# The first two column blocks of a convolution's input product share each quarter of x, in two accumulators

## The chip, the core and the metric

One Trainium2 chip, of which the kernel uses one core. The metric is the device time of one execution in microseconds (us), median of three runs. TensorE is written PE in the profile (PEld is its loading of weights), VectorE is DVE, ScalarE is ACT, GpSimd is POOL and SyncE is SP.

## What is computed

A trunk of two residual layers on x of 256 tokens by 2048 channels, all in float32. Layer 0 mixes tokens with a Conformer convolution, layer 1 with a state space; each is followed by a dense MLP. The change is in the first step of layer 0, `h @ w_in`, and in what surrounds it:

```python
def rms_norm(x, g):
    xf = x.astype(jnp.float32)
    y = xf * lax.rsqrt(jnp.mean(xf * xf, axis=-1, keepdims=True) + EPS)
    return (y * g.astype(jnp.float32)).astype(x.dtype)
...
def conv_module(h, w_in, b_in, dw, dw_b, ln_g, ln_b, w_out, b_out):
    u = h @ w_in + b_in
    a, gate = jnp.split(u, 2, axis=-1)
    v = a * jax.nn.sigmoid(gate)
    v = lax.conv_general_dilated(
        v, dw[:, None, :], window_strides=(1,),
        padding=[(CONV_WIDTH - 1, 0)],
        dimension_numbers=("NWC", "WIO", "NWC"),
        feature_group_count=D_MODEL) + dw_b
    v = layer_norm(v, ln_g, ln_b)
    v = jax.nn.silu(v)
    return v @ w_out + b_out
```

`w_in` is 2048 by 4096, and the depthwise convolution has 31 taps per channel.

## The kernel before

Every weight matrix is read once from HBM in steps of 1 MiB. A step lands in a tile `raw` (three buffers), and is split in two halves h = 0, 1, 2, ...: ACT writes the rounded part `hi` (line 118), and DVE, or POOL for the steps in `pool_lo`, the rest `lo` (line 125); there are four buffers of each. PE then makes three products per tile of weights (`mm_g`, lines 211 to 213: hi by the high part of x, hi by its low part, lo by its high part), so that the result is that of float32.

x comes in four quarters of 512 channels (`setup`). A quarter is transposed on PE (`xt`, line 254, two tiles of four transposes), scaled by the norm's weights on ACT and split on DVE into `hT` (lines 258 and 259). The RMS factor of the tokens is worked out from sums of squares (`junk`, `ssq`), raised to the power -0.5 on POOL, spread to all partitions by a product (`bc`, line 296), and applied after the product, in `gate`.

`conv_in` has 16 column blocks c of 128 + 128 columns (value and gate). A block needs 2048 channels, two steps, four halves and 96 products, in one accumulator `acc` of which there are two. Its end is `gate` (lines 446 to 448): DVE multiplies `acc` by the RMS factor, ACT makes the sigmoid `ga`, DVE writes v into `vT`, and `acc` is free. Blocks 0 to 11 then go through `depthwise`: 30 operations `cv` on DVE (line 829), the last of which writes `vT`. Blocks 12 to 15 (`PACKED`) do it on PE: v is copied in shifted form into `R` (for block 15 by 8 copies on DVE, line 470, and 8 on ACT, line 468), 32 small products make `pk` (line 484), and DVE finishes them. `centre` (line 569) takes a shift from four finished blocks at once, ACT squares them (`sq`), and PE adds both up into `stat` (line 539), from which `lst` and `tot` make the layer norm. Then comes `conv_out`.

The order on each engine is set when the program is built, by a scheduler that takes what is ready by its own estimate of times; `behind(ins)` puts one instruction after another, and `high_priority` brings one forward. On the chip each engine keeps that order and waits where an operand is missing. Transfers of x and of the weights are issued one behind the other on SP's queue (`fetch`, line 92), a quarter of x and a half step of weights in turn; the small vectors of the layer (`dwr`) are issued on POOL's queue behind `pow_ins`, so after the RMS factor.

```python
for n in range(NS):
    s = slice(n * 512, (n + 1) * 512)
    self.fetch(self.x[:, :, s], xv[:, :, s])
    self.load(n // 2, n % 2)
```

## Time and profile before

| | |
|---|---|
| median of three runs | 1987.88 us (1987.52 to 1989.23) |
| profiled execution | 1987.94 us, its span 1986.2 us |
| PE busy | 1966.6 us, 99% of the span |
| DVE busy | 1400.9 us, 71% |
| ACT busy | 952.1 us, 48% |
| POOL busy | 275.0 us, 14% |
| HBM read | 400.08 MB, 219 GB/s over the span |

The span counts from the first instruction; what lies outside it is 1.7 us. A row of the timeline gives the start in us from there, the time from the start to the end of what it merges, engine, line, operation, tiles and count; in brackets stands how long the engine was idle before, and what ended that. A matmul's printed duration holds its way through the array, so the pace of PE is read from the starts of neighbours. The stretch up to 230 us of the span is the one that the change touches: the first 38 us hold blocks 0 and 1, at 214 us block 15 ends, and at 236 us `conv_out` begins.

### The profile page before, as it was taken

The numbers are of one execution on the slowest core, as the hardware profiler recorded it, in microseconds if no ns is written. First come the engines' busy times: TensorE is split into PE (matmuls) and PEld (weight loads), VectorE is DVE, ScalarE is ACT, GpSimd is POOL, SyncE is SP. The second block draws the span as 40 slices with busy tenths as digits, with TensorE's granted clock in tenths as the row PEclk, the third lists the DMA queues.
The fourth block names the chain that finished last, engine by engine and source line by source line (L and its number), as shares of the span: only waits on it lengthen the run. The fifth ranks groups of instructions, "written<-read, shape, count | busy, mean of one in ns | idle before, by whom it ended". The sixth has DMA issues, their size and how long they took to land.

```text
span 1986.2 us, 28885 instructions
## 1 busy us (share of the span) xinstructions
PE 1966.6 (99%) x11604; PEld 1686.1 (85%) x11604; DVE 1400.9 (71%) x1903; ACT 952.1 (48%) x1179; POOL 275.0 (14%) x252
## 2 busy tenths in 40 slices
PE   8999999999999999999999999999999999999998
PEld 8999788888888888888888788888888888888887
DVE  6899798888777777777558847565555565655555
ACT  6444655544444544444445445454444454444444
POOL 3998300000000221222010000000000000000000
PEclk9999999999999999999999999999999999999999
DMA  8768458677686877877898865665656666666653
GB/s 225 192 184 219 135 185 267 205 227 244 201 255 196 215 230 251 264 247 239 319 308 296 304 216 185 191 191 190 191 191 191 191 191 191 190 213 191 191 191 128
DMA packets 317030, 428.49 MB, mean 216 GB/s; under 512 B 9761, under 2 KB 211553, under 8 KB 313537
## 3 DMA queue, kind: packets, MB, share of 16 engines
q1 hardware_dynamic: 301120, 384.85, 61.4%
q0 software_dynamic: 12352, 37.49, 6.3%
q10 hardware_dynamic: 3424, 4.30, 0.8%
q8 instruction: 91, 1.49, 0.3%
q14 instruction: 43, 0.35, 0.1%
HBM read 400.08 MB, written 34.91 MB: 219 GB/s over the span
## 4 chain that ended last, share of the span: by engine, by line
PE 95%; DVE 1%; DMA 1%; issue 1%; POOL 1%; SPq 0%; ACT 0%; ACTq 0%; POOLq 0%; DVEq 0%
PE acc L199 24%; PE acc L222 15%; PE acc L223 15%; PE acc L224 15%; PE acc L202 12%; PE acc L213 3%; PE acc L212 3%; PE acc L211 3%; PE pk L484 1%; DMA Vt<-Vd 0%; PE kp L1113 0%; SPq L92 0%; POOL lo L125 0%; PE xw L1254 0%; DMA raw<-in_conv_w_in_dram 0%
## 5 line engine op out<-in xcount | busy, mean ns | idle before, releaser
L118 ACT ACTIVATE hi<-raw 128x1024 fp32r<-128x1024 f32 x672 | 711.3, 1060 | 952.4 <-PE acc L224 507.2
L125 DVE TENSOR_TENSOR lo<-raw,hi 128x1024 fp32r<-128x1024 f32 x611 | 747.0, 1225 | 505.3 <-ACT hi L118 501.1
L199 PE MATMUL acc<-hT,hi 128*128 128x512 f32 x2048 | 514.4, 393 | 0.0
L199 PEld LDWEIGHTS acc<-hT,hi 128*128 128x128 f32 x2048 | 368.9, 189 | 68.0 <-issue 1.6
L222 PE MATMUL acc<-hi,rT 128*128 128x512 f32 x992 | 387.2, 391 | 0.0
L223 PE MATMUL acc<-lo,rT 128*128 128x512 f32 x992 | 386.4, 390 | 0.0
L224 PE MATMUL acc<-hi,rT 128*128 128x512 f32 x992 | 386.0, 389 | 0.0
L202 PEld LDWEIGHTS acc<-hT,lo 128*128 128x128 f32 x2048 | 279.6, 190 | 20.0
L202 PE MATMUL acc<-hT,lo 128*128 128x256 f32 x2048 | 286.4, 282 | 0.0
L222 PEld LDWEIGHTS acc<-hi,rT 128*128 128x128 f32 x992 | 186.3, 188 | 40.0 <-issue 1.6
L224 PEld LDWEIGHTS acc<-hi,rT 128*128 128x128 f32 x992 | 186.3, 188 | 38.7
L223 PEld LDWEIGHTS acc<-lo,rT 128*128 128x128 f32 x992 | 186.3, 188 | 38.1 <-issue 0.2
L125 POOL TENSOR_TENSOR lo<-raw,hi 128x1024 fp32r<-128x1024 f32 x60 | 142.9, 2402 | 31.9 <-ACT hi L118 31.8
L211 PE MATMUL acc<-hT,hi 128*128 128x256 f32 x512 | 145.8, 285 | 0.9 <-ACT hi L118 0.9
L212 PE MATMUL acc<-hT,hi 128*128 128x256 f32 x512 | 145.5, 285 | 0.3 <-DVE hT L259 0.3
L213 PE MATMUL acc<-hT,lo 128*128 128x256 f32 x512 | 145.3, 286 | 0.3 <-POOL lo L125 0.3
L829 DVE SCALAR_TENSOR_TENSOR cv<-vT,dw,cv 128x256 f32<-128x256 f32 x348 | 141.2, 481 | 2.2 <-ACT cv L527 1.7
L820 DVE TENSOR_TENSOR x<-x,acc 128x1024 f32<-128x1024 f32 (+1 forms) x72 | 83.6, 1161 | 28.1 <-PE acc L224 22.0
L211 PEld LDWEIGHTS acc<-hT,hi 128*128 128x128 f32 x512 | 98.6, 193 | 3.1 <-issue 1.6
L222 PE MATMUL acc<-hi,yT 128*128 128x512 f32 x256 | 101.1, 395 | 0.0
L223 PE MATMUL acc<-lo,yT 128*128 128x512 f32 x256 | 99.9, 390 | 0.6 <-DVE lo L125 0.6
L212 PEld LDWEIGHTS acc<-hT,hi 128*128 128x128 f32 x512 | 98.5, 193 | 2.2 <-issue 1.6
(280 smaller groups left out, 1722.5 us busy)
## 6 DMA issues: line engine op xcount, KB each, us to landing
raw<-in_mlp_w_up_dram SPq DMA_DIRECT2D x128, 1024.0 KB, 5.8
raw<-in_mlp_w_down_dram SPq DMA_DIRECT2D x128, 1024.0 KB, 5.2
raw<-in_ssm_w_glu_dram SPq DMA_DIRECT2D x32, 1024.0 KB, 5.5
raw<-in_conv_w_in_dram SPq DMA_DIRECT2D x60, 512.0 KB, 5.6
raw<-in_conv_w_out_dram SPq DMA_DIRECT2D x16, 1024.0 KB, 5.1
Vd<-bv POOLq DMA_DIRECT2D x16, 512.0 KB, 6.3
Md<-Kd POOLq DMA_DIRECT2D x32, 256.0 KB, 6.7
Wt<-Wd SPq DMA_DIRECT2D x8, 1024.0 KB, 9.4
```

The source lines that it names most:

```text
L118: self.nc.scalar.activation(hi, sl, AF.Copy)
L125: ins = eng.tensor_tensor(out=lo, in0=sl, in1=hi.bitcast(F32), op=ALU.subtract)
L199: mm(accs[m], lhsT=hi[:, kk, cs[m]], rhs=xT(k0 + kk), start=first and kk == 0, stop=False)
L202: mm(accs[m][:, 0:T], lhsT=lo[:, kk, cs[m]], rhs=xT(k0 + kk)[:, 0, :], start=False, stop=last and kk == 3)
L211: mm(accs[m], lhsT=hi[:, kk, c], rhs=x[:, 0, :], start=first and kk == 0, stop=False)
L212: mm(accs[m], lhsT=hi[:, kk, c], rhs=x[:, 1, :], start=False, stop=False)
L213: mm(accs[m], lhsT=lo[:, kk, c], rhs=x[:, 0, :], start=False, stop=last and kk == 3)
L222: mm(acc[:, b, :], lhsT=ak[:, 0, t], rhs=hi[:, kk, :], start=first and kk == 0, stop=False)
L223: mm(acc[:, b, :], lhsT=ak[:, 0, t], rhs=lo[:, kk, :], start=False, stop=False)
L224: self.mm_last = mm(acc[:, b, :], lhsT=ak[:, 1, t], rhs=hi[:, kk, :], start=False, stop=last and kk == 1)
L820: return self.nc.vector.tensor_tensor(out=out, in0=a, in1=b, op=op)
L829: return self.nc.vector.scalar_tensor_tensor(out=out, in0=a, scalar=s, in1=b, op0=op0, op1=op1)
```

## The change

Blocks 0 and 1 are no longer worked one after the other with the whole of x. Their four steps now hold one quarter of x's channels each, for block 0 in the first half and for block 1 in the second, so a quarter of x is used for 24 products into one accumulator and 24 into the other. Both accumulators stay open until the fourth quarter, and both gates follow then. From block 2 on nothing is different in the code.

With it, the first quarter of x and of block 0's weights come in two pieces each; transposing a quarter (`quarter`), the sums of squares (`sums`), the RMS factor (`norm`), and its spreading with the small vectors' transposes (`spread_norm`, `vectors`) are called from `run_steps` at set halves (`early`), behind the split before them; the vectors' transfers start when x's second quarter has landed (`go`) in place of the RMS factor; 8 products of `ones` and twice 3 of `ident` go ahead of the first product (`warm`, `keep_warm`); and ACT's tables are loaded by two one-column operations (`ld`).

```diff
-        for n in range(NS):
+        for p in range(2):
+            s = slice(p * 256, (p + 1) * 256)
+            self.fetch(self.x[:, :, s], xv[:, :, s])
+            self.load(0, 0, p)
+        self.load(0, 1)
+        for n in range(1, NS):
             s = slice(n * 512, (n + 1) * 512)
             self.fetch(self.x[:, :, s], xv[:, :, s])
-            self.load(n // 2, n % 2)
+            if n < NS - 1:
+                self.load(n)
...
+        warm = self.acc2("warm")[:, 0, 0:P]
+        for _ in range(8):
+            nc.tensor.matmul(warm, lhsT=self.ones, rhs=self.ones, start=True, stop=True)
...
-        for n in range(NS):
-            self.to_features(self.x, self.mix0, 4 * n, 4)
-        for n in range(NS):
-            self.sumsq(ssq, n, True)
-        self.rstdB = self.bcast_tok(self.rstd_tok(ssq))
+        for k in (0, 2):
+            self.spread = self.to_features(self.x, self.mix0, k, 2)
+            self.keep_warm(3, self.xt, warm)
...
+        self.early = {1: lambda: quarter(1), 3: lambda: quarter(2), 4: norm, 5: lambda: quarter(3), 6: spread_norm}
+        go = nc.gpsimd.tensor_copy(out=self.small.tile([P, 1], F32, tag="go", name="go", bufs=1), in_=self.x[:, 0, 512:513])
...
-            with self.behind(self.pow_ins):
+            with self.behind(go):
                 nc.gpsimd.dma_start(out=rows[r:r + n, :], in_=ap.rearrange("(k p) -> k p", p=P))
...
-        for c in range(KB):
+        for s in range(NS):
+            def consume(hi, lo, half, s=s):
+                if s == 0:
+                    st[half] = self.acc2()
+                A = st[half][:, :, 0:T]
+                hi, lo = (t.rearrange("p k h c -> p k (h c)") for t in (hi, lo))
+                self.mm_g([A[:, 0], A[:, 1]], self.hT, hi, lo, 4 * s, s == 0, s == NS - 1)
+                if s == NS - 1:
+                    self.gate(half, A)
+            self.add([w[:, 4 * s:4 * s + 4, :, c * P:(c + 1) * P] for c in range(2)], [P, 8, 2, P], consume)
+        for c in range(2, KB):
```

PE's first instructions in the kernel before (`mt` is the norm's weights, `xt` a tile of transposed x, `acc` the accumulator):

```order
L323 MATMUL mt<-ident,m_78 128x16
L254 MATMUL xt<-ident,x 128x128 x8
L211 MATMUL acc<-hT,hi 128x256
L212 MATMUL acc<-hT,hi 128x256
L254 MATMUL xt<-ident,x 128x128 x8
L213 MATMUL acc<-hT,lo 128x256
```

and in the changed one:

```order
L352 MATMUL warm<-ones 128x128 x8
L357 MATMUL mt<-ident,m_78 128x16
L276 MATMUL xt<-ident,x 128x128 x4
L211 MATMUL warm<-ident 128x128 x3
L276 MATMUL xt<-ident,x 128x128 x4
L211 MATMUL warm<-ident 128x128 x3
L233 MATMUL acc<-hT,hi 128x256
```

Products without data from x stand ahead of and between the transposes; after the last row shown eleven more products follow, and only then the eight transposes of x's second quarter, which stood behind the second product before.

At the other end of `conv_in` the code is the same, but the scheduler's order is not. DVE from block 14's v to the finish of block 14, before (`cv` are depthwise operations of blocks 10 and 11, those that write `vT` the last of a block; the line 569 is `centre` of blocks 8 to 11; pk_2723 and pk_2809 are the packed products of blocks 13 and 14; the line 446 opens the gate of block 15):

```order
L448 SCALAR_TENSOR_TENSOR vT<-acc,vecs,ga 128x256
L829 SCALAR_TENSOR_TENSOR cv<-vT,dw,cv 128x256 x20
L829 SCALAR_TENSOR_TENSOR vT<-vT,dw,cv 128x256
L829 SCALAR_TENSOR_TENSOR cv<-vT,dw,cv 128x256
L829 SCALAR_TENSOR_TENSOR vT<-vT,dw,cv 128x256
L569 TENSOR_TENSOR vT<-vT,shift 128x4x256
L829 SCALAR_TENSOR_TENSOR vT<-pk_2723,vecs,shift 128x256
L446 TENSOR_TENSOR acc<-acc,bcs 128x2x256
L448 SCALAR_TENSOR_TENSOR vT<-acc,vecs,ga 128x256
L470 COPY R<-vT 32x284 x8
L829 SCALAR_TENSOR_TENSOR vT<-pk_2809,vecs,shift 128x256
```

and in the changed kernel (lines 900, 640, 517, 519 and 541 are the same operations; pk_2753 and pk_2839 are of blocks 13 and 14):

```order
L519 SCALAR_TENSOR_TENSOR vT<-acc,vecs,ga 128x256
L900 SCALAR_TENSOR_TENSOR cv<-vT,dw,cv 128x256 x25
L900 SCALAR_TENSOR_TENSOR vT<-pk_2753,vecs,shift 128x256
L900 SCALAR_TENSOR_TENSOR cv<-vT,dw,cv 128x256 x4
L900 SCALAR_TENSOR_TENSOR vT<-vT,dw,cv 128x256
L900 SCALAR_TENSOR_TENSOR cv<-vT,dw,cv 128x256
L517 TENSOR_TENSOR acc<-acc,bcs 128x2x256
L900 SCALAR_TENSOR_TENSOR vT<-vT,dw,cv 128x256
L640 TENSOR_TENSOR vT<-vT,shift 128x4x256
L519 SCALAR_TENSOR_TENSOR vT<-acc,vecs,ga 128x256
L541 COPY R<-vT 32x284 x8
L900 SCALAR_TENSOR_TENSOR vT<-pk_2839,vecs,shift 128x256
```

One depthwise operation and `centre` moved in between the two halves of block 15's gate, and 34 depthwise operations in place of 26 stand between the gates of blocks 14 and 15.

ACT in the same place, before (`sq` of 128x1024 squares what `centre` made):

```order
L571 ACTIVATE sq<-vT 128x1024
L492 ACTIVATE sq<-vT 128x256
L118 ACTIVATE hi<-raw 128x1024
L447 ACTIVATE ga<-acc,vecs 128x256
L468 ACTIVATE R<-vT 32x284 x8
L492 ACTIVATE sq<-vT 128x256
```

and after:

```order
L563 ACTIVATE sq<-vT 128x256
L137 ACTIVATE hi<-raw 128x1024
L518 ACTIVATE ga<-acc,vecs 128x256
L642 ACTIVATE sq<-vT 128x1024
L539 ACTIVATE R<-vT 32x284 x8
L563 ACTIVATE sq<-vT 128x256
```

The square of four blocks moved from ahead of the split and the gate to between the gate and the copies into R. Behind the layer norm of layer 0 both programs have the same order on every engine.

## Rows read from the trace of the kernel before

**Rows 1.** The page: busy time by engine, and the chain that ended last
```profile
PE 1966.6 (99%) x11604; PEld 1686.1 (85%) x11604; DVE 1400.9 (71%) x1903; ACT 952.1 (48%) x1179; POOL 275.0 (14%) x252
PE 95%; DVE 1%; DMA 1%; issue 1%; POOL 1%; SPq 0%; ACT 0%; ACTq 0%; POOLq 0%; DVEq 0%
```
**Rows 2.** Timeline of PE, blocks 0 and 1: start, us, engine, line, operation
```profile
5.12 1.97 PE L254 MATMUL xt<-ident,x 128*128 128x128 f32 x8 [1.12 <-DMA x<-in_x_dram]
8.04 0.58 PE L211 MATMUL acc<-hT,hi 128*128 128x256 f32 x1 [0.95 <-ACT hi L118]
...
10.56 0.41 PE L211 MATMUL acc<-hT,hi 128*128 128x256 f32 x1
10.77 0.41 PE L212 MATMUL acc<-hT,hi 128*128 128x256 f32 x1
...
13.05 0.60 PE L254 MATMUL xt<-ident,x 128*128 128x128 f32 x4
...
13.61 0.63 PE L254 MATMUL xt<-ident,x 128*128 128x128 f32 x4
...
19.74 0.39 PE L212 MATMUL acc<-hT,hi 128*128 128x256 f32 x1 [0.33 <-DVE hT L259]
...
23.03 0.59 PE L296 MATMUL bc<-dg,ones 128*128 128x256 f32 x2
...
31.82 1.18 PE L353 MATMUL dwt<-ident,dwr 31*128 31x31 f32 x16
...
38.05 0.28 PE L213 MATMUL acc<-hT,lo 128*128 128x256 f32 x1
38.17 0.28 PE L211 MATMUL acc<-hT,hi 128*128 128x256 f32 x1
```
**Rows 3.** Timeline of ACT: what waits for the first transfers of x and weights
```profile
5.10 0.63 ACT L271 ACTIVATE junk<-x 128x512 f32<-128x512 f32 x1 [2.58 <-DMA x<-in_x_dram]
...
16.51 1.06 ACT L118 ACTIVATE hi<-raw 128x1024 fp32r<-128x1024 f32 x1 [0.43 <-DMA raw<-in_conv_w_in_dram]
...
25.43 2.01 ACT L118 ACTIVATE hi<-raw 128x1024 fp32r<-128x1024 f32 x2 [2.27 <-DMA raw<-in_conv_w_in_dram]
```
**Rows 4.** Busy time by stretch: start:end length, ACT, clock, DMA share, GB/s
```profile
27.00:28.00 1.00, 0.44 (x1) 1.00 1.09 204
```
**Rows 5.** Timeline of DVE: gates of blocks 0, 8, 14 and 15, centre, copies
```profile
35.03 0.48 DVE L448 SCALAR_TENSOR_TENSOR vT<-acc,vecs,ga 128x256 f32<-128x256 f32 x1 [3.44 <-ACT ga L447]
...
124.63 0.70 DVE L446 TENSOR_TENSOR acc<-acc,bcs 128x512 f32<-128x512 f32 x1 [0.49 <-PE acc L213]
...
199.22 0.70 DVE L446 TENSOR_TENSOR acc<-acc,bcs 128x512 f32<-128x512 f32 x1 [0.59 <-PE acc L213]
...
210.66 1.74 DVE L569 TENSOR_TENSOR vT<-vT,shift 128x1024 f32<-128x1024 f32 x1
...
214.52 0.70 DVE L446 TENSOR_TENSOR acc<-acc,bcs 128x512 f32<-128x512 f32 x1 [1.73 <-PE acc L213]
215.92 0.49 DVE L448 SCALAR_TENSOR_TENSOR vT<-acc,vecs,ga 128x256 f32<-128x256 f32 x1 [0.70 <-ACT ga L447]
216.44 4.03 DVE L470 COPY R<-vT 32x284 f32<-32x284 f32 x8
220.50 0.48 DVE L829 SCALAR_TENSOR_TENSOR vT<-pk,vecs,shift 128x256 f32<-128x256 f32 x1
```
**Rows 6.** Timeline of ACT and POOL at the end of block 15
```profile
214.46 1.06 ACT L118 ACTIVATE hi<-raw 128x1024 fp32r<-128x1024 f32 x1 [0.66 <-PE acc L212]
...
216.44 3.60 ACT L468 ACTIVATE R<-vT 32x284 f32<-32x284 f32 x8 [0.55 <-DVE vT L448]
...
208.93 2.39 POOL L125 TENSOR_TENSOR lo<-raw,hi 128x1024 fp32r<-128x1024 f32 x1 [0.46 <-ACT hi L118]
215.59 2.37 POOL L125 TENSOR_TENSOR lo<-raw,hi 128x1024 fp32r<-128x1024 f32 x1 [4.28 <-ACT hi L118]
```
**Rows 7.** Line 470: durations of its copies, ns min/median/max, first and last start
```profile
L470 DVE COPY R<-vT x8: 295/299/1689, 216.4 to 220.0; 32x284 f32<-32x284 f32 x8
```

More of the change, by code (lines that the diff above doesn't have):

```diff
@@ L97, in load @@
             self.table(*kind)
-        if not half:
+        if not (half or part):
             self.raws[i] = self.w.tile(shape, F32, tag="raw", name="raw", bufs=3)
@@ L101, in load @@
         nk = shape[1] // 2
+        if isinstance(view, list):
+            for v in (0, 1) if half is None else (half,):
+                for k in (slice(0, nk),) if part is None else (slice(part * nk // 2, (part + 1) * nk // 2),):
+                    for j in range(shape[2]):
+                        self.fetch(raw[:, v * nk + k.start:v * nk + k.stop, j, :], view[v][:, k, j, :])
+            self.loaded = i + 1
+            return
         k = slice(0, shape[1]) if half is None else slice(half * nk, half * nk + nk)
@@ L116, in split @@
         lo = self.w.tile([P, nk] + list(raw.shape[2:]), F32R, tag="lo", name="lo", bufs=4)
-        with self.tc.high_priority(offset=URGENT if urgent else 0):
-            self.nc.scalar.activation(hi, sl, AF.Copy)
+        if h == 0:
+            for k in (slice(0, nk // 2), slice(nk // 2, nk)):
+                with ExitStack() as order:
+                    for ins in self.spread if k.start else (self.ready,):
+                        order.enter_context(self.behind(ins))
+                    order.enter_context(self.tc.high_priority(offset=URGENT))
+                    self.hsplit(sl[:, k], hi[:, k], lo[:, k])
+            self.parts[h] = (hi, lo)
+            return self.low
+        order = ExitStack()
+        for ins in self.spread if h in (1, 3, 5, 7) else ():
+            order.enter_context(self.behind(ins))
+        with order, self.tc.high_priority(offset=URGENT if urgent else 0):
+            hi_ins = self.nc.scalar.activation(hi, sl, AF.Copy)
             eng = self.nc.gpsimd if i in self.pool_lo else self.nc.vector
@@ L126, in split @@
             self.lo_gate = None
+            self.given = (hi_ins, ins)
             if i in self.pool_lo:
@@ L323, in setup, with quarter, sums, norm @@
         nc.tensor.transpose(ps, m0, self.ident[0:KB, 0:KB])
-        nc.vector.tensor_copy(out=self.mix0, in_=ps)
+        with self.tc.high_priority(offset=2 * URGENT):
+            self.ready = nc.vector.tensor_copy(out=self.mix0, in_=ps)
         self.new_hT()
         ssq = self.new_ssq()
-        for n in range(NS):
-            self.to_features(self.x, self.mix0, 4 * n, 4)
-        for n in range(NS):
-            self.sumsq(ssq, n, True)
-        self.rstdB = self.bcast_tok(self.rstd_tok(ssq))
+        for k in (0, 2):
+            self.spread = self.to_features(self.x, self.mix0, k, 2)
+            self.keep_warm(3, self.xt, warm)
+        def quarter(n):
+            with ExitStack() as order:
+                for ins in self.given:
+                    order.enter_context(self.behind(ins))
+                self.spread = self.to_features(self.x, self.mix0, 4 * n, 4)
+            if n < NS - 1:
+                sums(n - 1)
+        def sums(*ns):
+            with self.behind(self.spread[0]), self.behind(self.spread[1]):
+                for n in ns:
+                    self.sumsq(ssq, n, True)
+        def norm():
+            sums(2, 3)
+            with self.tc.high_priority(offset=URGENT):
+                self.rstd = self.rstd_tok(ssq)
+        def spread_norm():
+            with self.tc.high_priority(offset=URGENT):
+                self.rstdB = self.bcast_tok(self.rstd)
+                with self.behind(self.dga):
+                    nc.scalar.activation(self.small.tile([P, 1], F32, tag="ld", name="ld"), self.ones[:, 0:1], AF.Sigmoid)
+            vectors()
+        self.early = {1: lambda: quarter(1), 3: lambda: quarter(2), 4: norm, 5: lambda: quarter(3), 6: spread_norm}
         dwr = self.blk_tile([P, D + P], name="dwr")
+        go = nc.gpsimd.tensor_copy(out=self.small.tile([P, 1], F32, tag="go", name="go", bufs=1), in_=self.x[:, 0, 512:513])
         rows, dwr = dwr[:, D:], dwr[0:TAPS, 0:D]
```

39 lines of the change are left out of this document (22 added, 17 removed).

## The prediction, made before the changed kernel ran

> **What bounds the kernel now.** I read the page first: PE is busy for 99% of the span and holds 95% of the chain that ended last [rows 1]. So time can be won only where PE waits, runs at its lower clock, or does work that can go. The timeline of PE shows where that is in the first 38 us [rows 2]. PE starts at 5.12, when x's first quarter has landed. Its products of 256 columns start 0.21 us apart at 10.56 and 0.12 us apart at 38.05: that is 1.2 GHz first and 2.4 GHz later, after some 7 us of transposes, a wait of 0.95 us and first products. It waits once more at 19.74, and block 2 begins at 38.17. From there to block 15's end at 214.5 it hardly waits. The timeline of DVE tells who else could bound this stage [rows 5]: at block 8's gate (124.63) DVE waited for PE by 0.49 us, at block 14's by 0.59, at block 15's by 1.73. Between the first two it was busy without a break, so DVE is within about a microsecond of being the bound. That decides what a gain at the start is worth.
>
> **The start.** Filling products, one-column table loads and early sums stand on engines that wait for data until 5 us and cost nothing there. What sets the new start is that, after twelve products, PE's order has the transposes of x's second quarter. In the queue that quarter ends the first 2 MiB (x 0.25, weights 0.25, x 0.25, weights 0.25, block 1's weights 0.5, x 0.5). The first 0.5 MiB had landed at 5.10 and 4 MiB at 16.51 [rows 3], so 1 MiB takes (16.51 - 5.10) / 3.5 = 3.26 us, and 2 MiB land at 5.10 + 1.5 x 3.26 = 10.0 us. The twelve products can start at about 7 us (they need x and weights of the first 1 MiB in parts) and take 2.6 us even at 0.21 each, so they are over, and PE waits until 10.0.
>
> From then on PE has, up to block 2: eight transposes, 180 of the 192 products, sixteen more transposes, `bc`, and the small vectors' transposes. Between the two groups of transposes at 13.05 and 13.61 stands one product, so four transposes take 0.56 - 0.12 = 0.44 us, 0.11 each. `bc` takes about 0.4, the small vectors 1.3 [rows 2]. Sum: 10.0 + 0.9 + 180 x 0.12 (21.5, at 0.1195) + 1.8 + 1.8 = 36.0 us, against 38.17. The **gain at the start is 2.1 us**, if PE waits nowhere else. It should not, by small margins. x's third quarter ends the first 3.5 MiB (about 15 us) and is wanted at 15.8; the fourth ends 5 MiB (19.8) and is wanted at 21.5. Both accumulators are now open to the end, so block 2 waits for block 0's whole gate; that ended at 35.51 before because of a table load and late vectors [rows 5], and now has its table and its vectors early: `bc` at 31.5, then copy, multiplication, ACT and v, each 0.4 to 0.7, put its end near 35.0.
>
> **The end of the stage.** The 2.1 us must still come out behind block 15. There the order of DVE and ACT is another one, and its price is in rows. Block 15's gate would open at 214.52 - 2.1 = 212.4. DVE is ready about then: from 124.63 to 199.22 it did 165 depthwise operations, now 167 (counted in the order), and from gate 14 to gate 15 eight more of 0.39 but `centre` less: 199.22 to 212.8 before, 1.5 us longer now, so 197.1 + 15.1 = 212.2.
>
> Then comes what is new. Before, from the gate at 214.52 it went on to v (215.92), copies on DVE until 220.47, on ACT until 220.04, and block 15's packed products could begin at about 220.5 [rows 5, 6]. Now one depthwise operation and `centre` lie between gate and v, and the square of it between ACT's gate and copies. How long `centre` takes hangs on POOL. At 210.66 it took 1.74 us and ended at 212.40, which is 1.08 behind POOL's `lo` (208.93 + 2.39 = 211.32). The first of the copies on line 470 took 1.69 us, the others 0.30 [rows 7], and ended at 218.13, right behind POOL's `lo` (215.59 + 2.37 = 217.96) [rows 6]. I read both as DVE being held until POOL has finished. The Trainium skill (SBUF — State Buffer, section "Who interferes with whom") says so: a DVE instruction with two SBUF inputs and a GpSimd instruction that reads SBUF exclude each other for the whole instruction, and the one that issued first blocks the other; the two rows agree.
>
> POOL's next `lo` starts 1.07 behind the gate (215.59 against 214.52; it follows ACT's split, which follows PE), so at 213.5. `centre` follows the gate by 0.60 and 0.52, so at 213.5 too. I take POOL to be first, by 0.05 us of these sums, and because any lateness of DVE is on its side. Then `centre` ends at 213.5 + 2.4 + 1.1 = 217.0, the square on ACT at 218.0 (1.0), the eight copies on ACT 3.6 later at 221.6, and DVE's, not held any more, are done before. Block 15's products begin at 221.5 in place of 220.5: 1.0 later. One statistics product (0.2) that stood among them is now ahead, and small waits behind it shrink by some 0.15, so about 0.65 stays. The layer norm and all that follows has the same order as before and depends on these products.
>
> **Sum.** Gain at the start 2.1, price of the new end 2.75, net +0.65 us on the profiled 1987.94: 1988.6, which is 0.06 above the median as that execution was, so **1988.5 us**. That is no change that can be told: about 0.2%, 4 us, is what a measurement of this kernel can tell from none.
>
> **Rivals.** (a) DVE gets `centre` in first. It then ends at 214.6, POOL's `lo` at 217.0, ACT's copies at 219.2; DVE's first copy is held until 217.1 and the last is done at 219.3, block 14's finish at 219.8, and the products begin at 220.0, 0.5 earlier than before, with the statistics product 0.7 to 0.8: 1987.2. For it: the two starts are a tie. Beyond it lies the case that the end costs nothing, 1985.8, which only an idle POOL would give.
>
> (b) The start gains little, since data come late. The small vectors' transfers move from 20 us to about 10 and run beside x. In the trace of before, ACT waited 2.27 us for weights at 25.43, and in the stretch from 27 to 28 the engines moved 204 GB/s [rows 3, 4], just when those vectors came. If x's third quarter is held as long, PE stands about 1.1 us at 16, and the gain is 1.0: 1989.6; with nothing gained, which is also the case that the change doesn't do what it says, 1990.7. For it: margins of about 1 us. Against it: only the third quarter and block 0's gate are near the edge.
>
> (c) Slower in earnest: the clock. PE stands from about 8.5 to 10.0, now and not before. If it goes on at 1.2 GHz and takes as long as before to rise, some 7 us from 10.0, eight transposes and 25 products cost 0.1 more each: 3.1 us, so 1991.6; a second wait of that kind at x's third quarter makes it 1994.7. It decides if products start 0.21 us apart behind 10 us. Against it: PE has then had products nearly without a break since about 1 us.
>
> **Chances.** The forecast 0.45, (a) with what lies beyond 0.26, (b) 0.22, (c) 0.07. Of (c) most, and a little of (b), is slower by over 0.2%; of (a) hardly anything is faster by so much, as the gain at the start is 2.1 and 4.0 would be needed. So faster 0.02, within 0.2% 0.92, slower 0.06. The range reaches from (a), less half a microsecond of its sums, to the end of (b): 1986.5 to 1990.9.
>
> **What would show it.** Right: second transposes at about 10.0, block 2's first product at 36.0, gate 15 on DVE at 212.4, a `centre` behind it of over 3 us that ends 1.1 behind POOL's `lo`, and block 15's packed products at 221.5. Wrong at the start: gaps on PE between 15 and 36 us whose releaser is a transfer of x or weights, or a gap ahead of block 2 that DVE ends. Wrong at the end: a `centre` of 1.1 us with POOL's `lo` behind it (a), or DVE's gate 15 not waiting for PE, which would mean that DVE has become the bound and that more of the gain is gone. Products 0.21 us apart after 10 us show (c).

## The result, and the profile after

| | before | after |
|---|---|---|
| median | 1988.18 us (1987.28 to 1989.23, 13 runs) | 1991.32 us (1990.43 to 1994.43, 13 runs) |
| profiled execution, its span | 1987.94, 1986.2 | 1991.70, 1989.9 |
| x's second quarter has landed | 8.29 | 11.64 |
| x's fourth quarter has landed | 14.62 | 24.91 |
| block 2's first product | 38.17 | 39.15 |
| block 15's first product | 199.02 | 200.31 |
| gate 15 on DVE | 214.52 | 215.81 |
| first `lst` | 225.05 | 229.13 |
| `conv_out`'s first product | 231.97 | 236.04 |

The changed kernel is slower: 1.0018 times the time before (95% interval 1.0010 to 1.0025), 3.1 us in the medians. The forecast was 1988.5, within 0.2% of before, and its range ended at 1990.9. All of the loss lies ahead of `conv_out`, in three pieces that add up in the profiled pair: 0.98 us at the start (39.15 - 38.17), 0.31 between blocks 2 and 15, 2.79 from block 15's first product to the first `lst` (28.82 against 26.03); 0.32 comes back later, on balance: 3.76, as 1991.70 - 1987.94. "Landed" is here when the last of the 16 DMA engines reports a transfer done, by the trace's semaphore events. The landings are of unlike amounts: the second quarter ends the first 1.5 MiB before and the first 2 MiB after, the fourth 3.5 and 5 MiB. (Ahead of the result `conv_out` was said to begin at 236 us. Its first product is at 231.97; 236.26 is where PE has waited for the last of its operands.)

The start, in the timeline of PE (columns as in [rows 2]):

```profile
11.68 1.09 PE L276 MATMUL xt<-ident,x 128*128 128x128 f32 x8 [1.76 <-DMA x<-in_x_dram]
12.53 0.36 PE L233 MATMUL acc<-hT,hi 128*128 128x256 f32 x1
12.73 0.28 PE L234 MATMUL acc<-hT,hi 128*128 128x256 f32 x1
12.85 0.28 PE L235 MATMUL acc<-hT,lo 128*128 128x256 f32 x1
...
25.05 0.30 PE L276 MATMUL xt<-ident,x 128*128 128x128 f32 x1 [1.21 <-DMA x<-in_x_dram]
...
39.15 0.28 PE L233 MATMUL acc<-hT,hi 128*128 128x256 f32 x1
```

Two waits end with a transfer of x: 1.76 us at the second quarter, 1.21 at the fourth. Products are 0.12 us apart from 12.73 on, so in this execution the clock is at 2.4 GHz early, which it was not before [rows 2]. What the transfers moved from 4 to 10 us, in the kernel before and then in the changed one (start:end length, the engines, the clock, the share of the DMA engines, GB/s):

```profile
4.00:10.00 6.00, 3.93 (x17) 3.53 (x18) 3.25 (x8) 3.86 (x9) 0.00 (x0) 1.00 1.09 337
```

```profile
4.00:10.00 6.00, 5.92 (x37) 5.28 (x36) 3.03 (x7) 3.29 (x7) 0.00 (x0) 1.00 0.90 243
```

243 GB/s in place of 337. (The clock of the first line is not to be read: that trace records the granted clock only from 12.1 us on, and its products stand 0.21 us apart until then.) In the kernel before, x's second quarter was the fourth transfer on SP's queue, and 16 engines reported it within 0.81 us of each other; here it is the ninth, and they are 2.47 us apart (9.17 to 11.64).

The end of the stage, DVE first, then POOL, then PE, which answer to [rows 5, 6]:

```profile
215.81 0.70 DVE L517 TENSOR_TENSOR acc<-acc,bcs 128x512 f32<-128x512 f32 x1 [0.20 <-PE acc L235]
216.41 0.47 DVE L900 SCALAR_TENSOR_TENSOR vT<-vT,dw,cv 128x256 f32<-128x256 f32 x1
216.92 3.43 DVE L640 TENSOR_TENSOR vT<-vT,shift 128x1024 f32<-128x1024 f32 x1
220.28 0.47 DVE L519 SCALAR_TENSOR_TENSOR vT<-acc,vecs,ga 128x256 f32<-128x256 f32 x1
```

```profile
216.88 2.39 POOL L144 TENSOR_TENSOR lo<-raw,hi 128x1024 fp32r<-128x1024 f32 x1 [4.27 <-ACT hi L137]
```

```profile
220.41 0.64 PE L610 MATMUL stat<-vT,ones 128*32 128x256 f32 x8 [1.05 <-DVE vT L640]
...
224.66 3.02 PE L555 MATMUL pk<-R,wpk 128*32 128x256 f32 x43 [0.20 <-ACT R L539]
...
229.13 0.49 PE L658 MATMUL lst<-q,stat 128*128 128x1 f32 x3
```

Gate 15 opens when PE is done; then `centre` takes 3.43 us and ends at 220.35, 1.08 behind POOL's `lo` (216.88 + 2.39 = 219.27). v comes 4.47 us behind the gate's start, where it was 1.40 [rows 5], and block 15's packed products start 8.85 us behind it.

### The profile page after: what moved, and what is told of

Same layout as the page of the kernel before. It is cut to its first block, busy times and chain, and to the rows that moved or that the text cites. A ratio compares the mean times of both kernels' runs of the same rounds, so it can differ in the third digit from the quotient of the medians.

```text
span 1989.9 us, 28956 instructions
## 1 busy us (share of the span) xinstructions
PE 1969.7 (99%) x11632; PEld 1687.9 (85%) x11632; DVE 1402.1 (70%) x1904; ACT 953.0 (48%) x1182; POOL 276.7 (14%) x253
## 4 chain that ended last, share of the span: by engine, by line
PE 95%; DVE 2%; DMA 1%; SPq 1%; issue 1%; POOL 0%; ACT 0%; ACTq 0%; POOLq 0%; DVEq 0%
PE acc L221 24%; PE acc L244 15%; PE acc L245 15%; PE acc L246 15%; PE acc L224 12%; PE acc L235 3%; PE acc L234 3%; PE acc L233 3%; SPq L92 1%; PE pk L555 1%; DMA x<-in_x_dram 1%; DMA Vt<-Vd 0%; PE kp L1184 0%; PE xt L276 0%; PE xw L1325 0%
## 5 line engine op out<-in xcount | busy, mean ns | idle before, releaser
L221 PEld LDWEIGHTS acc<-hT,hi 128*128 128x128 f32 x2048 | 368.9, 189 | 67.9 <-issue 1.2
L244 PE MATMUL acc<-hi,yT 128*128 128x512 f32 x256 | 101.1, 395 | 0.0
L234 PEld LDWEIGHTS acc<-hT,hi 128*128 128x128 f32 x512 | 98.2, 192 | 2.3 <-issue 2.1
L246 PE MATMUL acc<-hi,yT 128*128 128x512 f32 x256 | 99.7, 390 | 0.0
```

The costliest lines, as they stand in the source:

```text
L221: mm(accs[m], lhsT=hi[:, kk, cs[m]], rhs=xT(k0 + kk), start=first and kk == 0, stop=False)
L234: mm(accs[m], lhsT=hi[:, kk, c], rhs=x[:, 1, :], start=False, stop=False)
L244: mm(acc[:, b, :], lhsT=ak[:, 0, t], rhs=hi[:, kk, :], start=first and kk == 0, stop=False)
L246: self.mm_last = mm(acc[:, b, :], lhsT=ak[:, 1, t], rhs=hi[:, kk, :], start=False, stop=last and kk == 1)
```

## The experiments

The edits are against the changed kernel unless the text says otherwise. "End" is the time from block 15's first product to the first `lst`; both are read from the timeline of PE in each kernel's one profile. Ratios are to the kernel before on the same chip, with their 95% interval; a median alone is a single run.

| run | median, us | ratio | x's 2nd, 4th quarter landed | block 2 begins | end |
|---|---|---|---|---|---|
| changed | 1991.32 | 1.0018 (1.0010 to 1.0025) | 11.64, 24.91 | 39.15 | 28.82 |
| whole | 1992.76 | 1.0021 (1.0012 to 1.0030) | 10.27, 23.07 | 36.99 | 28.82 |
| x_pieces | 1996.45 | | 10.50, 23.21 | 43.43 | 26.92 |
| w_pieces | 1992.16 | | 10.16, 23.01 | 36.54 | 28.82 |
| go4 | 1990.16 | 1.0012 (1.0004 to 1.0021) | 11.47, 21.38 | 39.24 | 25.89 |
| go3 | 1992.01 | 1.0019 (1.0010 to 1.0028) | 11.42, 23.38 | 38.52 | 28.82 |
| go3_b | 1990.98 | | 11.17, 21.93 | 37.97 | 28.82 |
| go3_c | 1990.45 | | 11.14, 22.21 | 37.68 | 28.81 |
| lo_late | 1991.76 | 1.0024 (1.0015 to 1.0032) | 11.64, 23.99 | 39.25 | 28.82 |
| centre_first | 1989.38 | 1.0009 (0.9999 to 1.0018) | 11.32, 24.31 | 38.55 | 26.74 |
| lo_behind | 1991.19 | 1.0015 (1.0006 to 1.0024) | 11.24, 23.74 | 37.98 | 29.44 |
| no_fill | 1991.61 | 1.0016 (1.0008 to 1.0025) | 11.44, 24.32 | 38.83 | 28.82 |
| best2 | 1991.09 | 1.0016 (1.0007 to 1.0024) | 10.10, 22.93 | 36.83 | 29.78 |
| best5 | 1992.68 | 1.0022 (1.0013 to 1.0031) | 10.09, 23.20 | 36.72 | 28.89 |
| best6 | 1993.21 | 1.0025 (1.0016 to 1.0034) | 10.17, 22.91 | 36.43 | 30.52 |
| before_fill | 1996.07 | 1.0035 (1.0023 to 1.0046) | 8.37, 14.66 | 41.69 | 26.03 |
| before_fill_go3 | 1996.04 | 1.0035 (1.0022 to 1.0048) | 8.36, 14.74 | 41.14 | 26.03 |

None beats the kernel before; centre_first alone can't be told from it. All lie within 0.5% of it. "End" of best5 can't be compared with the others (see there).

### Why x comes late: the pieces

```diff
-        for p in range(2):
-            s = slice(p * 256, (p + 1) * 256)
-            self.fetch(self.x[:, :, s], xv[:, :, s])
-            self.load(0, 0, p)
-        self.load(0, 1)
+        self.fetch(self.x[:, :, 0:512], xv[:, :, 0:512])
+        self.load(0, 0)
+        self.load(0, 1)
```

> The changed kernel, but x's first quarter and block 0's first half step of weights come whole again, as in the kernel before (two issues of 256 KB and 512 KB in place of six of 128 and 256 KB); the order of DVE and its work stay those of the changed kernel. Theory, small pieces: in the changed kernel SP issues 1.5 MiB in 4.1 us and the transfers of the first 10 us run at 190 to 280 GB/s, against 260 to 356 before; whole, the first 2 MiB land at about 10.1 us (before: 10.06) in place of 11.64, PE's second transposes start at 10.2 in place of 11.68, block 2 begins 1.5 us earlier, at 37.7, and the time is 1989.8 us. Rival, the queue is late for another reason (the order of steps, the number of transfers behind): the second quarter still lands at 11.6 and the time stays at 1991.3. The wait of 1.2 us for x's fourth quarter and the loss of 2.8 us behind block 15 should stay under both.

The second quarter landed at 10.27, with the engines 1.04 us apart, and the transfers moved 320 GB/s from 4 to 10 us:

```profile
4.00:10.00 6.00, 4.40 (x32) 3.59 (x31) 2.18 (x6) 2.40 (x6) 0.00 (x0) 1.00 1.10 320
```

PE's second transposes, in the kernel with whole quarters:

```profile
10.31 0.98 PE L276 MATMUL xt<-ident,x 128*128 128x128 f32 x7 [0.35 <-DMA x<-in_x_dram]
```

Block 2 began 2.16 us earlier, more than expected, since the fourth quarter came earlier too and PE did not wait for it. The same 2.17 us were still there at `conv_out`'s first product (233.87). In this profile 1.4 us of it were lost again at 1068.5, where the clock fell (last section). The median, 1992.76, did not follow at all, so that whole quarters make the kernel faster is not shown by its time.

Two more runs kept one of the two splits each: x_pieces fetches x's two pieces and then the weights whole, w_pieces x whole and then the weights in pieces.

> The changed kernel with x's first quarter in two pieces, one behind the other, and block 0's first half step of weights whole behind them. Which of the pieces put the 16 DMA engines out of step: if it is those of x, the first and the last engine to land x's second quarter are 1.8 us or more apart (2.47 in the changed kernel, 1.04 with both whole) and it lands at 11 us or later; if it is those of the weights, about 1.0 apart, at 10.3. The order on DVE differs a little from the changed kernel's in blocks 2 to 6, so nothing is read from the time.

> The changed kernel with x's first quarter whole and block 0's first half step of weights in its four pieces of 128 KB behind it; the order of the engines is the changed kernel's. With x's pieces alone the last engine landed x's second quarter 1.20 us behind the first, at 10.50 us. If the weights' pieces put the engines out of step, the spread here is 1.8 us or more and the quarter lands at 11 us or later; if it takes pieces of x and of weights in turn, as in the changed kernel (2.47, 11.64), the spread here is about 1.1 and it lands at 10.4.

Neither split alone puts the engines out of step: the quarter landed at 10.50 (1.20 apart) and 10.16 (0.96). Over all profiles, the nine of kernels that fetch pieces of x and of weights in turn landed it at 11.14 to 11.64, with the engines 1.46 to 2.47 apart; the six others of the changed kernel's kind at 10.09 to 10.50, at most 1.20 apart. So it is the alternation that costs: 0.6 to 1.6 us, 1.3 between the medians of the two groups. The number of transfers alone does not explain it: with 5, 6 and 7 of them ahead of the quarter (whole, x_pieces, w_pieces) it landed at 10.27, 10.50 and 10.16, with 8 in the changed kernel at 11.64. What makes an engine fall behind there is open: the rows show it from x's second piece on (4.66 to 6.75 in the changed kernel), not why. (In x_pieces block 2 waited 4.49 us for block 0's gate: the scheduler had put 16 small operations on ACT ahead of `ga`. Its time says nothing on the pieces.)

### Why x comes late: the vectors

The copy on POOL that starts the vectors' transfers reads a column of x's second quarter in the changed kernel. go4 lets it read the fourth, go3 the third (1024:1025):

```diff
-        go = nc.gpsimd.tensor_copy(..., in_=self.x[:, 0, 512:513])
+        go = nc.gpsimd.tensor_copy(..., in_=self.x[:, 0, 1536:1537])
```

> The changed kernel, but the small vectors' transfers start when x's fourth quarter has landed, not its second. Theory, the vectors' transfers hold up x: the fourth quarter lands at about 21.5 us in place of 24.91, PE's wait of 1.21 us ahead of its transposes at 25.05 goes, block 2 begins 1.2 us earlier, at 37.9; the vectors land near 31, ahead of block 0's gate. Rival, the engines' queues have got out of step for good after the small pieces: the fourth quarter lands at 24 or later, and block 2 begins at 39.1 or later. The scheduler's order at the end of the stage is another one here: centre stands ahead of gate 15 on DVE, as in the kernel before. If the 2.8 us that are lost behind block 15 come from that order, block 15's last product to the first lst takes 10.9 us, as before (11.2 at most), not 13.6. Both theories right: 1987.7 us; only the vectors: 1990.1; only the order: 1988.9; none: 1991.3.

> The changed kernel, but the small vectors' transfers start when x's third quarter has landed (16.7 us), not its second (11.6); every engine keeps the changed kernel's order, the end of the stage included. Theory, the vectors' transfers hold up x's fourth quarter: they start some 5 us later, the quarter lands between 21.4 (where it landed with the vectors behind it) and 23, and PE's wait at 25.05 goes or falls to under 0.3; the vectors land near 27, ahead of block 0's gate; block 2 begins at 37.9 to 38.2 in place of 39.15, and the time is 1990.3 us. The 28.8 us from block 15's first product to the first lst stay. Rival, the fourth quarter is late because the engines are out of step since the small pieces: it lands at 24 or later, block 2 at 39, 1991.3.

With the vectors behind the fourth quarter, 3 MiB lie between the landings of the second and the fourth quarter and take 9.91 us (11.47 to 21.38), 3.3 per MiB, the rate that the prediction used. In the changed kernel the same 3 MiB take 13.27. The vectors' transfers thus hold up x by 3.4 us in this pair of profiles, of which PE saw 1.21; in the four other kernels that have the changed kernel's pieces and vectors (lo_late, centre_first, lo_behind, no_fill) the 3 MiB took 12.35 to 12.99, and PE waited for the fourth quarter by 0.93 us or less. SP issued that quarter at 14.73 and 14.59, so it was not issued late. The vectors' own 304 KB would be 1.0 us at this rate; why they cost more is open. It fits what the Trainium skill says of the two ways in (DMA: Bandwidth & Descriptors, section "SWDGE vs HWDGE vs iDMA"): transfers issued by GpSimd and those of the sync engine stand in different queues inside the same 16 engines, which go round between them. The trace agrees as far as it goes: it shows the 3.4 us, not the turns.

But go4 gained nothing at block 2. The vectors then landed at 32.51; in the scheduler's new order PE's spreading of the norm and the vectors' transposes began at 35.77 and 36.21 (34.69 and 35.12 in the changed kernel), and block 2 waited for the gate:

```profile
39.24 0.39 PE L233 MATMUL acc<-hT,hi 128*128 128x256 f32 x1 [1.66 <-DVE vT L519]
```

I had expected 37.9. go3 is the middle: no wait for x's fourth quarter in any of its three profiles, block 2 at 38.52, 37.97 and 37.68. Its order of work up to `conv_out` is the changed kernel's, and so is its end, 28.8.

### What the end costs: order and POOL

centre_first puts gate 15 behind `centre`. The scheduler then also moved ACT's square of four blocks ahead of the gate, and block 14's finish on DVE ahead of the copies, so it tests the order as a whole:

```diff
-            nc.vector.tensor_tensor(out=A, in0=A, in1=self.rstdB.broadcast_to([P, 2, T]), op=ALU.mult)
+            with self.behind(self.last_centre) if c == KB - 1 else nullcontext():
+                nc.vector.tensor_tensor(out=A, in0=A, in1=self.rstdB.broadcast_to([P, 2, T]), op=ALU.mult)
...
+        self.last_centre = nc.vector.tensor_tensor(out=v, in0=v, in1=self.shift.unsqueeze(1).broadcast_to([P, n, T]), op=ALU.subtract)
```

> The changed kernel, but the gate of block 15 on DVE is put behind centre (so one depthwise operation and centre stand ahead of it, as in the kernel before). Theory, the order costs the 2.8 us behind block 15: centre starts at about 216.0, ahead of POOL's lo, and takes 1.1 to 1.2 us; the gate starts at 217.2 in place of 215.81, v at 218.6 in place of 220.28, block 15's packed products at 222.7 in place of 224.66, and the time is 1989.3 us. Rival, DVE's backlog costs it whatever the order: centre, v and the copies end when they did, packed products at 224.5 and 1991.2 us.

```profile
215.52 1.23 DVE L641 TENSOR_TENSOR vT<-vT,shift 128x1024 f32<-128x1024 f32 x1
216.66 0.69 DVE L518 TENSOR_TENSOR acc<-acc,bcs 128x512 f32<-128x512 f32 x1
218.24 0.49 DVE L520 SCALAR_TENSOR_TENSOR vT<-acc,vecs,ga 128x256 f32<-128x256 f32 x1 [0.88 <-ACT ga L519]
```

```profile
216.25 2.75 POOL L144 TENSOR_TENSOR lo<-raw,hi 128x1024 fp32r<-128x1024 f32 x1 [4.28 <-ACT hi L137]
```

`centre` was first and took 1.23 us; now POOL's `lo` took 2.75 in place of 2.39. The end fell from 28.82 to 26.74 and the time to 1989.38, as expected (1989.3); eight of its eleven times lie below the fastest of the changed kernel, 1990.43. go4, which has `centre` ahead of gate 15 as the kernel before has, had 25.89.

lo_late was meant to take POOL's `lo` out of the way by putting it behind DVE's last copy:

> The changed kernel, but POOL's last lo (216.88 to 219.27 in its trace) is put behind DVE's last copy into R; nothing else moves. Theory, POOL holds centre: centre, which starts at 216.92, takes 1.1 to 1.2 us in place of 3.43, v starts at 218.1 in place of 220.28, block 15's packed products at 222.8 in place of 224.66, and the time is 1989.4 us. Rival, centre is slow by itself there, or what it waits for is not POOL: 3.4 us again, and 1991.3. A second rival, centre is short but ACT's square and copies behind it bind: v at 218.1, but packed products not before 224, and 1990.8 or more.

An ordering put across two engines had no effect here: POOL's `lo` started at 217.03, `centre` at 217.06 and took 3.44 us. The run tells nothing on POOL; it is the changed kernel once more (the same order on every engine up to `conv_out`), and its 1991.76 and its end of 28.82 agree with it. lo_behind does it by data:

```diff
+        if c == KB - 1:
+            self.lo_gate = nc.gpsimd.tensor_copy(out=self.small.tile([P, 1], F32, tag="go", name="go", bufs=1),
+                                                 in_=self.cblk(8)[:, 0:1])
```

> The changed kernel, and POOL's last lo waits for centre by data: a one-column copy on POOL reads what centre writes, and lo stands behind that copy. DVE's and ACT's orders stay. Theory, POOL holds centre: centre takes 1.2 us in place of 3.43, v starts 2.2 us earlier; lo begins about 0.3 behind centre's end, and now holds DVE's first copy into R until its own end, some 4.0 us behind centre's start plus 0.1 (so that copy takes 2 us or more); block 15's packed products begin about 1.5 us earlier against gate 15 (7.3 us behind it in place of 8.85), and the time is 1989.9 us. Rival, centre is slow by itself there: 3.4 us again, lo merely later, and 1991.4 or more.

```profile
215.75 1.23 DVE L643 TENSOR_TENSOR vT<-vT,shift 128x1024 f32<-128x1024 f32 x1
216.89 0.48 DVE L519 SCALAR_TENSOR_TENSOR vT<-acc,vecs,ga 128x256 f32<-128x256 f32 x1
217.40 4.49 DVE L544 COPY R<-vT 32x284 f32<-32x284 f32 x8
```

```profile
217.18 2.37 POOL L144 TENSOR_TENSOR lo<-raw,hi 128x1024 fp32r<-128x1024 f32 x1
```

Same order on DVE, same work, `lo` 0.2 us behind `centre`: 1.23 us in place of 3.43. So it is POOL that made `centre` slow. And as expected `lo` now held the copies: eight take 4.49, 2.0 more than in the changed kernel (2.48). The packed products began 7.94 us behind gate 15 (expected 7.3, changed 8.85). What they gained the clock took back: PE waited 2.54 us ahead of them, and ran at the lower clock behind that (below), so that the end was longer, 29.44, and the time 1991.19, not 1989.9. That is the order of rival (a), which the prediction had priced at 1987.2.

### What the fillers are worth

no_fill leaves out the 8 products of `ones` and the six of `ident`.

> The changed kernel without its filling products (8 of ones, twice 3 of ident). Theory, PE waits for data at the start and the fillers hide nothing but a clock that those waits cover: the first twelve products start 0.21 us apart in place of 0.12 and end by 10.7, ahead of x's second quarter; some 10 to 25 products behind it may run at the lower clock, 1.0 to 2.5 us, of which the wait of 1.2 us for x's fourth quarter takes back its part; block 2 at 39.1 to 40.4, the time 1991.3 to 1992.6. Rival, the fillers are what keeps the clock up through the wait of 1.8 us at x's second quarter: without them products are 0.21 us apart until 16 or later, block 2 at 41 or later, 1993 or more.

```profile
10.08 0.41 PE L234 MATMUL acc<-hT,hi 128*128 128x256 f32 x1
11.49 1.97 PE L276 MATMUL xt<-ident,x 128*128 128x128 f32 x8 [0.99 <-DMA x<-in_x_dram]
```

Without them products are 0.21 us apart until 14.7, and PE still waits for x's second quarter. Block 2 begins at 38.83 and the time is 1991.61, no different from 1991.32. In this kernel, where PE waits for data, the fillers are worth nothing.

Two runs put the 8 products of `ones` into the kernel before, the second with the vectors started at x's third quarter:

```diff
+        warm = self.acc2("warm")[:, 0, 0:P]
+        for _ in range(8):
+            nc.tensor.matmul(warm, lhsT=self.ones, rhs=self.ones, start=True, stop=True)
         self.mhalf = const.tile([P, NB], F32, name="mhalf")
```

> The kernel before with the eight filling products of ones and nothing else of the change. They lift the clock: products start 0.12 us apart from the first on, where before they were 0.21 apart until about 12 us. But the vectors' transfers still start with the RMS factor, land at 28.4 and 30.9, and PE's order has their transposes at the 123rd and 129th product (before: 144th and 149th). Theory, what the fillers win is lost waiting for the vectors: PE waits for them until about 31, 63 products follow, block 2 begins at 38.5 to 39.8 in place of 38.17, and the time is 1988.2 to 1989.5 us. Rival, the RMS factor and with it the vectors come earlier too, by what PE is earlier: block 2 at 36.5 to 37, 1986.3 to 1986.8. The end of the stage has the order of before and should cost what it did, 26.0 us from block 15's first product to the first lst.

> The kernel before with the eight filling products and with the vectors' transfers started when x's third quarter has landed (about 11.5 us) in place of the RMS factor; no shared quarters, no pieces. PE's order has the transposes of x's first two quarters ahead of the first product, and the vectors' behind the 95th to 100th. If both parts work: first product at about 9.2, then 192 products of 0.12, 16 transposes of 0.11, the spreading of the norm 0.4 and the vectors' transposes 1.3: 26.5 us of work, block 2 at 35.7 to 36.8 in place of 38.17, the order of the end as before (26.0 us to the first lst), and 1985.6 to 1986.7 us, faster than the kernel before. Rival, the vectors' transfers hold up x's fourth quarter or the next weights by 2 us or more, as in the changed kernel: block 2 at 38 or later, 1987.9 or more.

Both were slower by 0.35%, and both my theories were wrong:

```profile
8.42 1.97 PE L254 MATMUL xt<-ident,x 128*128 128x128 f32 x8 [2.18 <-DMA x<-in_x_dram]
...
16.59 0.41 PE L213 MATMUL acc<-hT,lo 128*128 128x256 f32 x1
16.80 0.41 PE L211 MATMUL acc<-hT,hi 128*128 128x256 f32 x1
```

The scheduler put the transposes of two quarters ahead of the first product, PE waited 2.18 us for the second, and from there to 17.7 ran at 1.2 GHz (granted clock 0.50 from 8 to 16), longer than in the kernel before, where products reach the 0.12 us at 12.2. Block 2 began 3.5 us later. Fillers ahead of a wait did not keep the clock up through the wait. This profile is the fastest of its six executions, 1991.31, so it explains 3.4 of the some 8 us by which the median is longer than that of the kernel before. The profile of before_fill_go3, 1996.36, shows what the slower ones may have in addition: 5.4 us were lost between block 2 and block 15, where POOL held the first `centre` (next but one section).

### Putting the findings together

best2 is whole with gate 15 behind the last depthwise operation, `centre` between gate and v, its square behind ACT's copies, and POOL's last `lo` behind DVE's last copy. best5 is w_pieces with centre_first and with POOL's addition into x later; best6 is the same without centre_first.

> The changed kernel with the first quarter and weights whole, as in the run that had that alone, and with the end of the stage put in order: gate 15 behind the last depthwise operation, centre between gate and v, its square on ACT behind the copies into R, and POOL's last lo behind the last copy on DVE. Both theories together: block 2 at 37.0; centre 1.2 us with POOL idle; block 15's packed products 6 us behind gate 15, as before the change (8.85 in the changed kernel), and from block 15's first product to the first lst 26.0 us, as before (28.8 in the changed kernel). With block 15's start at 198.1, lst at 224.1 to 224.3, 0.8 earlier than before the change, and 1987.2 us. Rival, the backlog of DVE: gate 15 does not start within 0.6 us of PE's last product of block 15, and lst comes at 225.5 or later, 1988.5. A wait of over 1.5 us that drops the clock in some executions can add 1.5 us to either.

> The changed kernel with x's first quarter whole (block 0's weights in pieces), with POOL's addition of the bias into x three halves later, so that it does not stand beside the first centre, and with gate 15 behind centre. Start theory: block 2 at 36.6 (39.15 in the changed kernel, 38.17 before). Theory of the tie: the first centre takes 1.2 us in the profile, and the times form one group. End: 26.7 us from block 15's first product to the first lst, as in the run with gate 15 behind centre. Together 0.6 us ahead of the kernel before: 1987.4 us, and 1989.0 if the clock drops once. Rival, another tie or wait takes the place of those removed: times in two groups again, or 1989.5 or more.

> The same without the order of gate 15: the scheduler itself now puts v and the copies into R ahead of centre. Centre's square then comes late for the sums on PE; 26.0 to 26.8 us from block 15's first product to the first lst, block 2 at 36.6, 1986.9 to 1987.5 us. Rival, PE waits over 1.5 us for the copies with nothing to do and its clock drops: 28 us or more, 1988.5.

The starts came as expected (36.83, 36.72, 36.43), 1.3 to 1.7 us ahead of the kernel before. The ends did not: in all three PE waited for the copies or sums with nothing to do, 1.90, 1.95 and 4.01 us, and ran at the lower clock afterwards. In best5 the first `lst` stands ahead of the last 24 packed products, so that its 28.89 is too good: from block 15's first product to `conv_out`'s it took 38.18 us, against 35.73 in the changed kernel and 32.94 in the kernel before. In the kernel before, the statistics products of four blocks and block 14's packed products fill the time until block 15's packed products.

### Two groups of times

The times of go3 lie at 1989.8 to 1990.2 (four), 1993.6 to 1994.6 (four), and three between. Its profile fell into the upper group, and there the first `centre`, of blocks 0 to 3, was held (DVE, then POOL):

```profile
108.72 6.17 DVE L640 TENSOR_TENSOR vT<-vT,shift 128x1024 f32<-128x1024 f32 x1
```

```profile
109.06 2.41 POOL L462 TENSOR_TENSOR x<-x,bo 128x1024 f32<-128x1024 f32 x1
111.42 2.39 POOL L144 TENSOR_TENSOR lo<-raw,hi 128x1024 fp32r<-128x1024 f32 x1
```

> The run with the vectors behind x's third quarter, once more. Theory of the tie: if its time is in the lower group (below 1991), the first centre took 1.2 us and POOL's addition 3.2; if in the upper (above 1993), centre took about 6.2 and the addition 2.4. Rival: the group does not go with it.

> As the run before it, a third time: the lower group of times goes with a first centre of 1.2 us, the upper with one of 6.2.

go3_b (1990.98), DVE and then POOL:

```profile
108.27 1.22 DVE L640 TENSOR_TENSOR vT<-vT,shift 128x1024 f32<-128x1024 f32 x1
```

```profile
108.61 3.17 POOL L462 TENSOR_TENSOR x<-x,bo 128x1024 f32<-128x1024 f32 x1
```

Both new runs were below 1991, both had the short `centre` and the addition of 3.2 us. The two instructions start 0.34 us apart in either case; who is held differs. When it is DVE, it is held by two POOL instructions in a row and loses 5 us, and `conv_out` begins at 238.50 in place of 234.97: 3.0 us from the hold, 0.55 from the start, as block 2 began 0.55 later. w_pieces, at 1992.16, shows the long one too (6.16). The kernel before has no such tie: its first `centre` (105.18, 1.68 us) is held by one `lo` that has been running since 103.39; it ends 1.08 us behind that one (105.78), and POOL's next `lo` starts only at 106.70. before_fill_go3 does have one (DVE, POOL, then PE): three POOL instructions in a row held `centre`, which ended 1.09 behind the last of them (112.94), and the clock fell in PE's wait for it.

```profile
106.16 7.87 DVE L573 TENSOR_TENSOR vT<-vT,shift 128x1024 f32<-128x1024 f32 x1
```

```profile
105.89 2.40 POOL L404 TENSOR_TENSOR x<-x,bo 128x1024 f32<-128x1024 f32 x1
108.25 4.69 POOL L125 TENSOR_TENSOR lo<-raw,hi 128x1024 fp32r<-128x1024 f32 x2
```

```profile
114.08 1.08 PE L543 MATMUL stat<-vT,ones 128*32 128x256 f32 x8 [3.79 <-DVE vT L573]
```

## Why the prediction was wrong

**The start** (forecast gain 2.1, measured loss 0.98) is where it failed, in two terms.

*x's second quarter at 10.0.* The step took the landing from the rate of the kernel before and counted the bytes ahead of it. The bytes were right: in the kernel before, 2 MiB had landed at 10.06. What failed is the assumption that pieces in turn move at the same rate; the second transposes came at 11.68, and whole quarters brought them to 10.31. That is 1.68 of the 3.15 us.

*x's fourth quarter at 19.8.* The sum let the vectors' transfers cost x nothing, though they move to its side; they cost it 3.4 us here, 2.4 or more in the other profiles. This is rival (b), with the right mechanism (PE stands, and x or weights release it), at the fourth quarter and not the third: 1.21 us more of the 3.15. But I priced it at 1.1 us and closed it at "nothing gained", 1990.7, and put the end of the range there. No row excluded a loss. The rest, 0.26, was not taken apart.

What the prediction called a gain is there, in part: with x's first quarter whole, block 2 began at 36.99 and 36.54 (whole, w_pieces), against the forecast of 36.0.

**DVE and gate 15** came as argued: the gate followed PE's last product (wait 0.20 us), DVE was ready 0.2 ahead. Block 15 opened 3.41 later than the forecast 212.4: 3.15 from the start, 0.26 between block 2 and here, where PE's one wait ended by another engine is 0.88 us, for POOL's `lo` at 134.85.

**The end** was forecast at 2.75 us, and was 2.79 (13.32 from gate 15 to `lst`, against 10.53). Each step is in the rows above: a `centre` of over 3 us, its end 1.08 behind POOL's `lo`, the packed products 8.85 behind the gate where I had 9.1. centre_first shows what the order costs as a whole, lo_behind that POOL's hold is what lengthens `centre`. POOL's `lo` and `centre` started 0.04 us apart, so rival (a) lost by as little as the prediction said. lo_behind is that rival, built, and it did not pay: 1991.19 in place of (a)'s 1987.2, since PE's wait and the lower clock behind it took what the packed products gained.

A first `centre` of 1.22 us stretches POOL's addition from 2.41 to 3.17, a late one waits for POOL. This is the rule that the Trainium skill states (SBUF — State Buffer, "Who interferes with whom"): a DVE instruction with two SBUF inputs and a GpSimd instruction that reads SBUF keep each other out. These rows agree, in both directions. That the one which issued first wins could not be read from the starts: 0.34 us apart in go3 and in go3_b, with different winners. Of the prediction's two rows only `centre` is such an instruction. The copies into R have one input, and that POOL holds them too is shown by the rows alone: 4.49 us for eight beside `lo`, 2.48 without.

**Rival (c)**, the clock, did not decide in the profile: products are 0.12 us apart from 12.73. It was there in others, though (last section).

**Range and chances.** 1991.32 lies 0.4 above the range and 0.16% above the median before, inside the 0.2% on which 0.92 stood; the two right-hand cases, (b) and (c), had 0.29 together, and the true one was both (b) and the forecast's own price of the end.

## What to carry to other kernels

A landing time is worked out from bytes only if the transfers keep their size, their order and their company: pieces of two streams in turn cost 1.4 us over 2 MiB here, and 304 KB of small rows on another queue (in transfers of 8 to 248 KB) 2.4 to 3.4 us over 3 MiB. A hold by POOL costs most where DVE's operation and POOL's start close together (`centre` took 3.43 and 6.17 us in place of 1.22) and little where POOL is nearly done (1.68), so a change that moves a stage by a microsecond can turn a tie that was won into one that is lost, far from the place it edits; look for such ties first. And a stretch in which PE has filler work of its own (statistics, packed products) should be left its order: each of three rearranged ends met a wait and a lower clock.

## What was not expected of the hardware

**A wait in mid-run can halve the clock behind it.** The clock fell behind waits of PE, but the same wait did not always do it. The lower clock followed waits of 1.66 us (go4, at 39.24), 1.83 (whole, at 1068.5), 1.90 and 0.36 (best2), 1.95 and 0.45 (best5), 2.05 (lo_late, at 11.68), 2.18 (before_fill), 2.54 (lo_behind), 3.79 (before_fill_go3, at 114.08), 4.01 (best6) and 4.49 (x_pieces, at 43.43), and two rows of shorter ones: 1.33 and 0.64 (before_fill_go3, until 10.25), and 1.48, 0.37 and 0.33 (x_pieces, until 10.54). It did not follow waits of 1.76 (the changed kernel at 11.68), 1.82 (best2 at 1069.3), 1.85 and 1.88 (go3 at 11.46 and 114.95), 1.86 (go4 at 11.52), 1.87 (centre_first at 11.37, w_pieces at 112.96) and 1.89 (lo_behind at 11.29), nor one of 1.50 near 1068 in most kernels. In best6 it fell a second time, at 229.9, where PE's longest wait had been 0.48 us. In go4, the granted clock by stretch (the third number from the end) and the pace of PE:

```profile
36.00:40.00 4.00, 2.34 (x25) 1.97 (x24) 3.17 (x7) 3.00 (x8) 4.00 (x2) 1.00 1.07 285
40.00:44.00 4.00, 4.00 (x23) 4.00 (x23) 2.07 (x5) 3.82 (x14) 0.23 (x1) 0.57 0.66 188
44.00:48.00 4.00, 4.00 (x35) 4.00 (x35) 4.00 (x11) 2.31 (x3) 2.53 (x2) 1.00 0.40 100
```

```profile
40.18 0.28 PE L234 MATMUL acc<-hT,hi 128*128 128x256 f32 x1
...
41.10 0.41 PE L233 MATMUL acc<-hT,hi 128*128 128x256 f32 x1
41.32 0.41 PE L234 MATMUL acc<-hT,hi 128*128 128x256 f32 x1
...
44.19 0.28 PE L234 MATMUL acc<-hT,hi 128*128 128x256 f32 x1
```

23 products in the four microseconds from 40, and 35 in the next four: at 0.12 us each, 1.4 us lost. A term for a wait of PE near 2 us should have that much added to its upper end. In lo_late the loss was hidden by the wait for x's fourth quarter (block 2 at 39.25 against 39.15).

**Scatter is a finding.** The changed kernel's times spread over 4.0 us and those of the kernel before over 2.0. A tie lost at the first `centre` (3.0 us between block 2 and block 15) and the lower clock (1.4) are both large enough to be in that spread. That they make it is not shown: go3's three profiles went with the groups of its times, and the profile of the changed kernel has neither.
